# A fifth pair of gate and up products by Strassen's scheme, and ScalarE's casts and first SiLU set one product later

## Chip, core and metric

One NeuronCore of a Trainium2 chip runs the whole model in one launch. The metric is the device time of one execution in microseconds, the median of the timed executions.

Engine names as in the profile: PE is TensorE (matmuls; PEld its weight loads), DVE is VectorE, ACT is ScalarE, POOL is GpSimd, SP is SyncE, which issues loads. Each engine takes its instructions in the order in which the program gives them to it.

## What is computed

Two layers on a sequence of 512 tokens with 1024 features. Each layer is a token mixer (causal pooling in layer 0, differential attention in layer 1), a residual sum with layer norm, a SwiGLU feed-forward, and again a residual sum with layer norm. Only the feed-forward is touched here:

```python
D_FF = 2816
def _swiglu(x, w_gate, w_up, w_down):
    return (jax.nn.silu(x @ w_gate) * (x @ w_up)) @ w_down

x = _layernorm(ALPHA * x + _swiglu(x, w_gate[i], w_up[i], w_down[i]), ln_ffn_g[i], ln_ffn_b[i])
```

All data are float32.

## The kernel before

**Three products for one.** Every operand is split into a high part (ScalarE's cast to the matmul's format) and a low part (VectorE's subtraction of that from the original). A product is high x high + high x low + low x high, three matmuls.

**Gate and up.** The 2816 hidden features are 22 blocks of 128, taken as 11 pairs (k = 0 to 10; block k and block k + 11). A pair needs gate and up for two blocks. It is computed in one of two ways:

- *plain* (function `plain`, once per block): gate and up each take 8 blocks of the inner dimension x 3 matmuls on 512 columns, 96 matmuls for a pair.
- *Strassen* (function `strassen`, pairs listed in `SPLIT`): the pair is a product of 2 x 2 blocks and is done with seven half-size products instead of eight, each of 2 x 4 x 3 = 24 matmuls on 256 columns, 168 for a pair. They come in the order P1, Q5, P6, Q3, P7, P2, Q4. P1, P6, P7 and Q4 add up in bank A of PSUM, Q5 and Q3 in bank C, P2 stands in bank B. Partial results are taken out between products: ScalarE copies P1 to a buffer (L814), Q5 to `second` (L816), P6 to `first` (L818), VectorE subtracts Q3 (L820) and P7 (L822) and adds P2 to the buffer of P1 (L824). ScalarE applies SiLU to that buffer (L825) and to bank A after Q4 (L828); VectorE multiplies with `first` and `second` (L832, L834). The next product that adds to a bank waits until the copy out of it is done. The buffers (`sg`) alternate between two.

**Weights.** A pair has four raw weight tiles of 512 KB, loaded by SP into five buffers (`raw`). A Strassen pair needs seven weight operands: VectorE makes four of them by sums of raw tiles (L552). Then every operand, seven or, for a plain pair, four, is cast (ScalarE, L555) and gets its low part (VectorE, L558); they stand in six pairs of buffers (names g_16h, g_16l and so on, numbered in the order of products; pair 4 begins at g_16). `ahead` after each product prepares the weights some products in front, in the order of the list `steps`.

**Work behind.** Generators in the list `behind` are advanced one step after each product by `catch_up`. There are two kinds:

- `sum_terms` (`weight_sums` starts one per pair, at the places in the tuple of `plain` and at the end of every Strassen pair): sums of blocks of the down weights on VectorE (L657, L658), then two stores to scratch memory by ScalarE's DMA queue (L662), and then GpSimd's loads of later terms (L651, L652).
- `sum_hidden` (once per pair): four VectorE instructions that add and subtract parts of the finished hidden blocks into `u` (L683 to L686), ScalarE's cast of `u` (L687), in the next step VectorE's low part (L689), then a store to scratch (L691).

**Down.** The product with the down weights uses the seven Strassen products over all pairs; its operands come from the hidden blocks and the scratch memory.

Of the kernel before, what the change touches and what calls it, by code (L numbers as in the profile page):

```python
# [43 lines left out]
RAWS = 5  # L44
HALF = FB // 2
DOWN = ("P1", "Q5", "P6", "Q3", "P7", "P2", "Q4")
SPLIT = (4, 6, 7, 9)
GATE = ("P1", "Q5", "P6", "Q3", "P7", "P2", "Q4")
PAIRS = [(0, 2), (2, 2), (4, 2), (6, 2), (8, 2), (10, 1)]

# [2 lines left out]
def trunk(ctx, tc, x, wall, pscale, lam_p, subln, table, lng, lnb, band, first, onehot, out):  # L53
# [395 lines left out]
    def ffn(layer, late):  # L449
# [5 lines left out]
        with tc.tile_pool(name=f"ffn{layer}", bufs=1) as fp:  # L455
# [221 lines left out]
            def sum_hidden(k):  # L677

                first, second = hid[:, k, :256], hid[:, k, 256:]
                a12, a22 = hid[:, k + HALF, :256], hid[:, k + HALF, 256:]  # L680
                u = fp.tile([P, 2, 256], F32, tag="u", name=f"u{layer}_{k}", bufs=1)
                v = fp.tile([P, 2, 2, 256], F32R, tag="v", name=f"v{layer}_{k}", bufs=2)
                tt(u[:, 0, :], first, second, op=ALU.subtract)  # L683
                tt(second, second, a22, op=ALU.subtract)
                tt(u[:, 1, :], a12, first, op=ALU.subtract)
                tt(u[:, 1, :], u[:, 1, :], second, op=ALU.add)  # L686
                nc.scalar.copy(v[:, :, 0, :], u)  # L687
                yield
                tt(v[:, :, 1, :], u, v[:, :, 0, :].bitcast(F32), op=ALU.subtract)  # L689
                yield  # L690
                nc.scalar.dma_start(out=ssum[:, :, :, k, :], in_=v.bitcast(F32))  # L691
# [65 lines left out]
            def plain(f):  # L757
                k = f // 2
                j = index[k] + 2 * (f % 2)
                a = (bank(f"g{layer}_{f}"), bank(f"u{layer}_{f}"))  # L760
                for i in range(2):
                    product(a[i], j + i, 0, S)
                    ahead(j + i + 5)
                    if f >= 3:
                        next(sums, None)
                    catch_up()
                gated(order[f], *a)
                if f < SB:
                    affine(n - 1, f)
                if f in (3, 5, 7, 11, 17):  # L770
                    weight_sums()
                if f == 3:
                    load_terms(3)
                if f % 2:
                    behind.append(sum_hidden(k))

            def strassen(k):
# [12 lines left out]
                def both(t):  # L790
                    return t.rearrange("p (f t) -> p f t", f=2)
# [4 lines left out]
                for j, p in enumerate(GATE):  # L796
# [15 lines left out]
                    if p == "P1":  # L812
                        g0 = tile_of(0)
                        nc.scalar.copy(both(g0), acc)  # L814
                    elif p == "Q5":
                        nc.scalar.copy(second, acc)  # L816
                    elif p == "P6":
                        nc.scalar.copy(first, acc)  # L818
                    elif p == "Q3":
                        tt(first, acc, first, op=ALU.subtract)  # L820
                    elif p == "P7":
                        tt(second, second, acc, op=ALU.subtract)  # L822
                    elif p == "P2":
                        tt(both(g0), acc, both(g0), op=ALU.add)  # L824
                        nc.scalar.activation(g0, g0, AF.Silu)  # L825
                    else:
                        g1 = tile_of(1)
                        nc.scalar.activation(both(g1), acc, AF.Silu)  # L828
                    ahead(index[k] + j + 6)
                    catch_up()  # L830
                    if p == "P2":
                        tt(first, both(g0), first, op=ALU.mult)  # L832
                    elif p == "Q4":
                        tt(second, both(g1), second, op=ALU.mult)  # L834
                weight_sums()
                behind.append(sum_hidden(k))
# [515 lines left out]
```

## Time and profile before

| | us |
|---|---|
| timed runs | 970.91, 968.00, 967.26; median 968.0 |
| profiled execution | 971.13, of which the span of its instructions is 969.2 |
| PE busy | 950.4 (98% of the span) |
| DVE busy | 722.7 (75%) |
| ACT busy | 462.6 (48%) |
| granted TensorE clock, mean | 0.996 of full speed |
| pairs 4 to 10 of gate and up | 131.6 to 279.6 in layer 0, 705.9 to 853.9 in layer 1 |

The profile shows, for every instruction, its start and length, the idle time of its engine before it and what ended that. Three kinds of view are used: groups of waits (who waited for whom, total, times, longest), the chain of work that ended last (followed back from the last instruction to what released it), and busy time by stretch. A row of the last has the stretch in us from the span's start, its length, busy time and count of PE, PEld, DVE, ACT and POOL, the granted clock, the busy share of the DMA engines and GB/s.

### The profile page before, as it was taken

How to read it: one execution, taken by the hardware profiler on the slowest of the kernel's cores; microseconds unless marked ns; L12 is line 12 of the kernel's file. 1: busy time of each engine (PE TensorE's matmuls, PEld its weight loads, DVE VectorE, ACT ScalarE, POOL GpSimd, SP SyncE). 2: the span in 40 equal slices, each digit the busy share in tenths (PEclk: the TensorE clock that was granted, in tenths of full speed). 3: DMA queues.
4: the chain of work that ended last, by engine and by line, in shares of the span. 5: the costliest groups of instructions: out<-in, count | busy, mean ns of one | idle time of the engine just before them, and what ended most of it. 6: DMA issues, size and time to landing. Idle time of an engine off the chain costs nothing.

```text
span 969.2 us, 14409 instructions
## 1 busy us (share of the span) xinstructions
PE 950.4 (98%) x5550; PEld 838.2 (86%) x5550; DVE 722.7 (75%) x1069; ACT 462.6 (48%) x754; POOL 120.5 (12%) x151
## 2 busy tenths in 40 slices
PE   8999999999999999999999999999999999999995
PEld 8898898998988888988888888998898989888884
DVE  6859976786668687688787677779776885577687
ACT  5753343343354456656556553733342543354460
POOL 4311211110000201000000000311211110001102
PEclk9999999999999999999999999999999999999998
DMA  8298887883967974323242222496996884787942
GB/s 220 86 291 269 300 260 254 250 273 125 304 225 236 346 260 153 115 78 86 78 141 76 66 88 87 119 315 210 280 290 198 255 287 145 244 265 272 346 151 87
DMA packets 82242, 197.04 MB, mean 203 GB/s; under 512 B 14804, under 2 KB 26196, under 8 KB 82174
## 3 DMA queue, kind: packets, MB, share of 16 engines
q1 hardware_dynamic: 43052, 115.35, 35.2%
q0 software_dynamic: 15520, 46.14, 17.1%
q10 hardware_dynamic: 23602, 34.63, 10.2%
q8 instruction: 43, 0.70, 0.3%
q14 instruction: 25, 0.20, 0.1%
HBM read 159.38 MB, written 36.72 MB: 202 GB/s over the span
## 4 chain that ended last, share of the span: by engine, by line
PE 89%; DVE 7%; ACT 2%; issue 1%; POOL 1%; POOLq 0%; DVEq 0%; ACTq 0%
PE P L870 13%; PE A L805 7%; PE Q L870 6%; PE g L126 5%; PE u L127 5%; PE g L127 5%; PE u L125 5%; PE u L126 5%; PE g L125 5%; PE C L805 4%; PE s L1060 2%; PE B L805 2%; PE v L125 2%; PE v L126 2%; PE v L127 2%; PE q L126 1%
## 5 line engine op out<-in xcount | busy, mean ns | idle before, releaser
L584 DVE TENSOR_TENSOR hid<-sg,u 128x512 f32<-128x512 f32 x28 | 19.2, 686 | 64.7 <-PE u L127 41.5
L687 ACT CAST v<-u 128x512 fp32r<-128x512 f32 x22 | 13.7, 621 | 103.9 <-DVE u L686 103.9
L107 ACT CAST xs<-hid 128x512 fp32r<-128x512 f32 (+1 forms) x60 | 34.7, 581 | 23.0 <-DVE hid L719 23.0
L108 DVE TENSOR_TENSOR xs<-hid,xs 128x512 fp32r<-128x512 f32 (+1 forms) x60 | 38.4, 641 | 7.8 <-ACT xs L107 7.8
L217 ACT ACTIVATE y<-pt,bT,gT 128x128 f32<-128x128 f32 x96 | 36.0, 455 | 16.8 <-PE pt L212 15.8
L1070 ACT ACTIVATE p<-p,mn 128x128 f32<-128x128 f32 (+3 forms) x64 | 35.4, 553 | 14.9 <-DVE mn L1065 14.9
L552 DVE TENSOR_TENSOR raw<-raw,raw 128x1024 f32<-128x1024 f32 x32 | 39.1, 1220 | 0.3
L651 POOL DMA_DIRECT2D b<-in_wall x20 | 14.0, 705 | 171.8 <-DMA tsum<-b 124.3
L711 POOL DMA_DIRECT2D xs<-ssum x24 | 17.4, 725 | 140.1 <-PE Q L870 118.9
L651 POOL DMA_DIRECT2D hid<-in_wall x24 | 18.8, 827 | 91.6 <-DMA tsum<-hid 46.1
L108 POOL TENSOR_TENSOR sql<-sq,sqh 128x512 fp32r<-128x512 f32 x7 | 9.1, 1294 | 165.3 <-ACT sqh L107 165.3
L1065 DVE CUSTOM_DVE_ANT_0 p<-s,bias 128x128 f32<-128x128 f32 (+3 forms) x64 | 28.1, 485 | 0.0
L174 POOL TENSOR_SCALAR rs<-mv 128x1 f32<-128x1 f32 x16 | 8.1, 509 | 159.6 <-DVE mv L172 159.6
L108 DVE TENSOR_TENSOR xt<-y,xt 128x512 fp32r<-128x512 f32 x24 | 16.1, 685 | 15.4 <-ACT xt L107 15.3
L814 ACT COPY sg<-A 128x512 f32<-128x512 f32 x8 | 4.7, 586 | 42.3 <-PE A L805 42.3
L166 DVE BATCH_NORM_STATS2 st<-res 128x6 f32<-128x512 f32 x32 | 22.2, 695 | 1.1
L652 POOL DMA_DIRECT2D hid<-in_wall x12 | 14.8, 1232 | 54.7 <-DMA hid<-in_wall 49.4
L108 DVE TENSOR_TENSOR heads<-k,heads 128x512 fp32r<-128x512 f32 x8 | 5.5, 693 | 20.2 <-ACT heads L107 20.2
L583 ACT ACTIVATE sg<-g 128x512 f32<-128x512 f32 x28 | 16.6, 592 | 5.6 <-PE g L127 5.6
L600 ACT CAST xs<-hid 128x1024 fp32r<-128x1024 f32 x8 | 8.4, 1052 | 21.3 <-DVE hid L617 11.6
L1084 DVE SCALAR_TENSOR_TENSOR p<-p,sm,p 128x128 f32<-128x128 f32 (+3 forms) x32 | 17.6, 551 | 1.1
L1060 PE MATMUL s<-heads 64*128 64x256 f32 (+2 forms) x192 | 17.9, 330 | 0.0
(1088 smaller groups left out, 3614.3 us busy)
## 6 DMA issues: line engine op xcount, KB each, us to landing
raw<-in_wall SPq DMA_DIRECT2D x122, 512.0 KB, 5.5
r<-tsum SPq DMA_DIRECT2D x40, 512.0 KB, 4.4
hid<-in_wall POOLq DMA_DIRECT2D x36, 512.0 KB, 7.5
b<-in_wall POOLq DMA_DIRECT2D x30, 512.0 KB, 7.4
r<-in_wall SPq DMA_DIRECT2D x30, 512.0 KB, 5.8
tsum<-hid ACTq DMA_DIRECT2D x24, 512.0 KB, 5.9
ssum<-v ACTq DMA_DIRECT2D x22, 512.0 KB, 6.8
tsum<-b ACTq DMA_DIRECT2D x20, 512.0 KB, 3.0
```

The source lines that it names most:

```text
L107: nc.scalar.copy(dst_h, src)
L108: (low or nc.vector).tensor_tensor(dst_l, src, dst_h.bitcast(F32), op=ALU.subtract)
L125: nc.tensor.matmul(acc, ah, bh, start=start, stop=False)
L126: nc.tensor.matmul(acc, ah, bl, start=False, stop=False)
L127: nc.tensor.matmul(acc, al, bh, start=False, stop=stop)
L217: nc.scalar.activation(y[:, k, :], pt[:, k * P : (k + 1) * P], AF.Identity, bias=bT[:, n, kk : kk + 1], scale=gT[:, n, kk : kk + 1],)
L552: tt(t, raws[pair[0]], raws[pair[1]], op=ALU.add)
L651: nc.gpsimd.dma_start(out=t[:, j], in_=src[:, j])
L805: nc.tensor.matmul(o, w[:, c], x[:, kk, :], start=p in ("P1", "Q5", "P2") and f + kk + e == 0, stop=p in ("Q4", "Q3", "P2") and (f, kk, e) ...
L870: nc.tensor.matmul(accs[s], x[:, k, r], y[:, c], start=first and k == 0 and e == 0, stop=last and k == m - 1 and e == 2, skip_group_check= ...
L1060: nc.tensor.matmul(accs[c][:, :wide], a[r, qs], b[r, :wide], start=i == 0, stop=i == 2)
L1070: nc.scalar.activation(p, p, AF.Exp, bias=mn[:, q, c : c + 1], scale=-1.0, accum_out=sm[:, q, c : c + 1],)
```

## The change

One more pair is computed by Strassen's scheme, and the pairs are chosen anew: 4, 5, 6, 8, 9 instead of 4, 6, 7, 9. Plain pairs behind pair 3 are then 7 and 10 instead of 5, 8 and 10. The places of `weight_sums` follow, so that there is still one start per pair. `sum_hidden` gets one more step: ScalarE's cast of `u` is issued one `catch_up` behind VectorE's four instructions. In `strassen` the first SiLU is issued behind the `ahead` and `catch_up` of P2, and the first multiply one product later, just before the second.

```diff
-SPLIT = (4, 6, 7, 9)
+SPLIT = (4, 5, 6, 8, 9)
...
                 tt(u[:, 1, :], a12, first, op=ALU.subtract)
                 tt(u[:, 1, :], u[:, 1, :], second, op=ALU.add)
+                yield
                 nc.scalar.copy(v[:, :, 0, :], u)
                 yield
                 tt(v[:, :, 1, :], u, v[:, :, 0, :].bitcast(F32), op=ALU.subtract)
...
                 if f < SB:
                     affine(n - 1, f)
-                if f in (3, 5, 7, 11, 17):
+                if f in (3, 5, 7, 15):
                     weight_sums()
...
                     elif p == "P2":
                         tt(both(g0), acc, both(g0), op=ALU.add)
-                        nc.scalar.activation(g0, g0, AF.Silu)
                     else:
                         g1 = tile_of(1)
                         nc.scalar.activation(both(g1), acc, AF.Silu)
                     ahead(index[k] + j + 6)
                     catch_up()
                     if p == "P2":
+                        nc.scalar.activation(g0, g0, AF.Silu)
+                    elif p == "Q4":
                         tt(first, both(g0), first, op=ALU.mult)
-                    elif p == "Q4":
                         tt(second, both(g1), second, op=ALU.mult)
```

How the order on the engines moves is shown at a joint, where one Strassen pair follows another. Before there is one joint per layer (pairs 6 and 7), after the change there are three (4-5, 5-6, 8-9).

ScalarE at the joint of pairs 6 and 7, before: from the cast of pair 7's sixth weight operand to the copy of its P6.

```order
L555 CAST g_39h<-raw_1804 128x1024
L555 CAST g_40h<-raw_1578 128x1024
L814 COPY sg_7_0_2001<-A_7_1974 128x512
L662 DMA tsum_536<-b_7_1612 128x2x512 x2
L687 CAST v_6_2013<-u_6_2012 128x2x256
L816 COPY hid_534<-C_7_1975 128x2x256
L555 CAST g_41h<-raw_1836 128x1024
L818 COPY hid_534<-A_7_1974 128x2x256
```

ScalarE at the joint of pairs 4 and 5 after the change, the same piece (line numbers are one higher here):

```order
L555 CAST g_28h<-raw_1417 128x1024
L555 CAST g_29h<-raw_1221 128x1024
L815 COPY sg_5_0_1615<-A_5_1588 128x512
L662 DMA tsum_536<-b_5_1226 128x2x512 x2
L817 COPY hid_534<-C_5_1589 128x2x256
L555 CAST g_30h<-raw_1449 128x1024
L688 CAST v_4_1627<-u_4_1626 128x2x256
L819 COPY hid_534<-A_5_1588 128x2x256
```

The cast of the earlier pair's `u` stood ahead of the copy of Q5 out of bank C; now it stands behind that copy and a weight cast, just ahead of the copy of P6.

VectorE at the end of pair 6, before: from the low part of a weight operand of pair 7 over the addition of P2 (L824) and the two multiplies to the sum of down weights.

```order
L558 TENSOR_TENSOR g_36l<-raw_1578,g_36h 128x1024
L824 TENSOR_TENSOR sg_6_0_1754<-B_6_1729,sg_6_0_1754 128x512
L832 TENSOR_TENSOR hid_534<-sg_6_0_1754,hid_534 128x2x256
L552 TENSOR_TENSOR raw_1578<-raw_1578,raw_1804 128x1024
L558 TENSOR_TENSOR g_38l<-raw_1694,g_38h 128x1024
L834 TENSOR_TENSOR hid_534<-sg_6_1_1961,hid_534 128x2x256
L657 TENSOR_TENSOR b_7_1612<-b_7_1612 128x512
```

VectorE at the end of pair 4 after the change, the same piece:

```order
L558 TENSOR_TENSOR g_25l<-raw_1221,g_25h 128x1024
L825 TENSOR_TENSOR sg_4_0_1368<-B_4_1343,sg_4_0_1368 128x512
L552 TENSOR_TENSOR raw_1221<-raw_1221,raw_1417 128x1024
L558 TENSOR_TENSOR g_27l<-raw_1307,g_27h 128x1024
L834 TENSOR_TENSOR hid_534<-sg_4_0_1368,hid_534 128x2x256
L835 TENSOR_TENSOR hid_534<-sg_4_1_1574,hid_534 128x2x256
L657 TENSOR_TENSOR b_5_1226<-b_5_1226 128x512
```

The first multiply moved behind a weight sum and a low part, next to the second multiply.

## The prediction

> **What bounds the kernel now.** I read the page first: its span, its engine shares, the chain that ended last.
>
> ```profile
> span 969.2 us, 14409 instructions
> PE 950.4 (98%) x5550; PEld 838.2 (86%) x5550; DVE 722.7 (75%) x1069; ACT 462.6 (48%) x754; POOL 120.5 (12%) x151
> PE 89%; DVE 7%; ACT 2%; issue 1%; POOL 1%; POOLq 0%; DVEq 0%; ACTq 0%
> ```
>
> TensorE sets the end nearly everywhere, so only two things can pay: fewer columns on TensorE, or removal of a place where it waits. Next I cut the gate and up stage of the first FFN at the first matmul of each pair from 4 to 10 (a view of busy time by stretch; the first two numbers are the stretch and its length, then busy PE, PEld, DVE and ACT).
>
> ```profile
> 131.63:151.94 20.31, 20.31 (x170) 20.19 (x168) 16.29 (x21) 9.64 (x12) 2.69 (x3) 1.00 1.02 324
> 151.94:173.73 21.79, 21.79 (x99) 18.03 (x97) 12.63 (x16) 6.32 (x8) 2.72 (x3) 1.00 0.74 230
> 173.73:194.04 20.31, 20.31 (x170) 20.19 (x168) 18.27 (x22) 9.02 (x11) 2.70 (x3) 1.00 0.79 237
> 194.04:215.75 21.71, 20.42 (x171) 20.22 (x170) 17.39 (x23) 10.74 (x14) 2.71 (x3) 1.00 0.81 277
> 215.75:237.53 21.78, 21.78 (x98) 18.02 (x97) 12.62 (x16) 6.32 (x8) 0.00 (x0) 1.00 0.49 156
> 237.53:257.85 20.32, 20.32 (x170) 20.20 (x169) 16.04 (x20) 8.70 (x11) 2.35 (x3) 1.00 0.78 275
> 257.85:279.63 21.78, 21.78 (x98) 18.02 (x97) 11.84 (x17) 8.27 (x12) 0.00 (x0) 1.00 0.76 233
> sum 148.02, PE 146.73 PEld 134.90 DVE 105.08 ACT 58.87 POOL 13.13; mean PE 20.96 PEld 19.27 DVE 15.01 ACT 8.41 POOL 1.88
> ```
>
> The last row is the sum of the same seven pairs of the second FFN; the first FFN's seven lengths add up to 148.00 us. Plain pairs (5, 8, 10) take 21.78. Strassen pairs take 20.31, except pair 7, which directly follows another Strassen pair and takes 21.71. What pair 7 loses is in the waits of TensorE and in the chain:
>
> ```profile
> PE C L805 <- ACT hid L816: 2.6, 2, 1.3
> ```
>
> ```profile
> 179.64 2.88 PE A L805 x24
> 182.52 3.06 PE C L805 x24
> ...
> 185.67 0.06 DVE hid L820
> ...
> 194.66 0.64 ACT sg L825
> ...
> 202.51 0.43 DVE u L686
> ...
> 202.97 0.03 ACT v L687
> ...
> 203.50 0.59 ACT hid L816
> ...
> 204.13 3.14 PE C L805 x24
> ```
>
> Product Q3 adds to bank C, so it must wait until ScalarE has copied Q5's result out of it (L816). In ScalarE's queue L816 stands behind the cast L687, which waits for VectorE's L686. VectorE reaches L686 late at a joint of two Strassen pairs, and for 18.5 us (185.67 to 204.13) the chain runs over VectorE. The same wait is small elsewhere: Q3 of pair 6 takes 3.06 instead of 2.88. So an undisturbed Strassen pair would be 7 x 2.88 = 20.16 us.
>
> **The change part by part.** Line numbers are those of before; from L687 on, the changed file is one higher (the second product's multiply L834 becomes L835), the first SiLU L825 becomes L832 and the first multiply L832 becomes L834.
>
> *The fifth Strassen pair.* 96 matmuls of 512 columns (21.78 / 96 = 227 ns each) give way to 168 of 256 (2.88 / 24 = 120 ns each). Per layer 21.78 - 20.16 = 1.62 us less TensorE time, in two layers 3.24. The Strassen pairs become 4, 5, 6, 8, 9.
>
> The Trainium skill, "TensorE: Matmul & The Clock Gate", section "Back-to-back issue gap", gives N / 2.4 + 2.5 ns for a warm matmul. An estimate by that is 96 x 215.8 - 168 x 109.2 = 2.37 us per pair, so 4.7 us in place of 3.24 and a total near 959.2 us. This trace has about 13 ns per matmul above the columns' time instead of 2.5, so the 72 additional matmuls eat more of the gain; the rows above decide.
>
> *The cast L687 one product later.* It now stands behind L816 (second ScalarE listing above). L816 then waits only for Q5's end and for the two DMA issues ahead of it. The wait of pair 7 goes, 21.71 - 20.16 = 1.55 us per layer, 3.10 in two, and the small ones of the other three, 0.15 + 0.15 + 0.16 = 0.46, 0.92 in two. Both assume that nothing else is late in its place, and there are now three joints per layer (4-5, 5-6, 8-9) where there was one. So the joint must be walked with VectorE's own rows.
>
> ```profile
> 185.67:207.38 21.71, 20.42 (x171) 20.22 (x170) 19.36 (x24) 11.26 (x15) 2.71 (x3) 1.00 0.80 245
> ```
>
> ```profile
> 185.67 0.69 DVE L820 TENSOR_TENSOR hid<-C,hid 128x512 f32<-128x512 f32 x1 [1.09 <-PE C L805]
> ...
> 189.81 0.68 DVE L822 TENSOR_TENSOR hid<-hid,A 128x512 f32<-128x512 f32 x1
> ...
> 193.94 0.68 DVE L824 TENSOR_TENSOR sg<-B,sg 128x512 f32<-128x512 f32 x1
> 195.32 0.69 DVE L832 TENSOR_TENSOR hid<-sg,hid 128x512 f32<-128x512 f32 x1 [0.70 <-ACT sg L825]
> 195.93 1.22 DVE L552 TENSOR_TENSOR raw<-raw,raw 128x1024 f32<-128x1024 f32 x1
> 198.20 0.68 DVE L834 TENSOR_TENSOR hid<-sg,hid 128x512 f32<-128x512 f32 x1
> ```
>
> The first row is the cycle from pair 6's L820 to pair 7's: VectorE works 19.36 us in it. The changed joint holds the same 24 instructions, so TensorE's 20.16 us per pair leaves VectorE 0.80 us of slack per joint: tight, but a lag does not add up from joint to joint. With time from the start of the earlier pair, L820 starts at 11.64 (Q3 ends at 4 x 2.88 = 11.52, and the rows start 0.1 later). By the distances of the rows L822 runs from 15.78 to 16.46, and Q4 wants bank A at 6 x 2.88 = 17.28: 0.8 to spare. L824 ends at 20.59.
>
> *SiLU and multiplies later.* VectorE's 0.70 us wait for the SiLU at the joint goes, because it now does a weight sum and a low part (195.93 to 198.20, 2.27) before the first multiply, which then ends at 20.59 + 2.27 + 0.61 = 23.47; the SiLU is ready at about 20.6 + 0.6 = 21.3. This is worth nothing by itself on TensorE; it is what brings L686 forward: its end came 4.74 behind the start of L834 (198.20 to 202.94), at 29.2, and comes at 23.47 + 4.74 = 28.2. It adds one wait: the next pair's copy of P1 (L814) writes the buffer that the first multiply reads, since there are two of them. L814 stood here:
>
> ```profile
> 197.26 1.05 ACT L555 CAST g_40h<-raw 128x1024 fp32r<-128x1024 f32 x1 [0.55 <-DVE raw L552]
> 198.21 0.58 ACT L814 COPY sg<-A 128x512 f32<-128x512 f32 x1
> 200.25 0.37 ACTq L662 DMA_DIRECT2D tsum<-b  x1
> ```
>
> The cast ahead of it needs a buffer that the next pair's P1 frees at 23.04, so it runs from 23.1 to 24.1 and L814 from 24.1 to 24.7, after the multiply's 23.47 anyway. The next P6 needs bank A free at 20.16 + 5.76 = 25.92: 1.2 to spare. Behind L814 stand the DMA issues, which wait for VectorE's L658 and went 2.05 behind the start of L834 (198.20 to 200.25), so at 25.5; then L816, which waits for Q5 (25.92) and ends at 26.7; Q3 starts at 28.80: 2.1 to spare. Then L687 waits for L686 (28.2), and L818 behind it waits for P6's end (28.80) anyway; P7 starts at 31.68. L820 of the next pair is wanted at 31.80, and VectorE is free for it at 11.64 + 19.36 = 31.00. So nothing takes the wait's place, by 0.8 us. Where two joints follow each other (4-5-6) the second repeats the first. After pairs 6 and 9 the SiLU also falls behind a cast, but there VectorE has the work of a plain pair.
>
> *Loads.* The sums read new raw tiles just behind L820. After a plain pair they were issued only a little earlier:
>
> ```profile
> 179.67 0.33 SPq L97 DMA_DIRECT2D raw<-in_wall  x1
> ```
>
> ```profile
> 187.53 1.23 DVE raw L552
> ```
>
> ```profile
> raw<-in_wall SPq DMA_DIRECT2D x1, 512.0 KB, 7.1
> raw<-in_wall SPq DMA_DIRECT2D x7, 512.0 KB, 8.0
> b<-in_wall POOLq DMA_DIRECT2D x3, 512.0 KB, 10.1
> ssum<-v ACTq DMA_DIRECT2D x1, 512.0 KB, 15.4
> ```
>
> The second sum of pair 6 starts at 187.53, and its tile (issued at 179.67, 7.1 us to landing) came 0.8 us before. The rows below it are medians of raw loads around pair 4, of term loads around pairs 6 and 7, and the longest 512 KB transfer around pair 4. The changed joints 4-5 and 8-9 have this tile in the same place (joint 5-6 has its tiles long before). At 8.0 the sum would start 0.1 late; a lateness up to 0.8 is swallowed by bank A's margin. So a landing costs TensorE from 8.7 us on, one us per us, at four joints. I take the raw loads' own row: no cost. Far end: 15.4, (15.4 - 8.7) x 4 = 27 us.
>
> The Trainium skill, "DMA: Bandwidth & Descriptors", section "Issuing engines are not separate DMA queues", says that transfers of all queues interleave on the same 16 engines; the raw loads' 7.1 beside 8.0 in the busier stretch (DMA share 1.02) fit that. By that rule this price hangs on the scratch writes in flight beside, not on SP.
>
> *End of the stage.* VectorE waits there for the last weight terms:
>
> ```profile
> 264.56 0.69 DVE L657 TENSOR_TENSOR b<-b 128x512 f32<-128x512 f32 x1 [2.52 <-DMA b<-in_wall]
> ...
> 279.90 0.69 DVE L584 TENSOR_TENSOR hid<-sg,u 128x512 f32<-128x512 f32 x1 [4.19 <-PE u L127]
> ```
>
> Those terms are loaded once the sum before them has been stored. That sum followed the end of pair 8 (237.53); now it follows the Strassen pair 8, which starts at 131.63 + 3 x 20.16 + 21.78 = 213.9, by 24.1 us: 238.0. So the terms come when they came before, or little earlier, and TensorE is 3.6 us ahead: the wait grows from 2.5 to between 4 and 6. It holds up the next weights and operands of the down stage on VectorE, which were finished 4.19 us before the last row's wait ended, about when TensorE enters the down stage, and of which TensorE takes one item per 2.7 us (12 matmuls of 227 ns). The reserve of 4.19 shrinks to between 1 and 3. No cost; without that cover up to 2 us per layer.
>
> **The sum.** Per layer 5 x 20.16 + 2 x 21.78 = 144.36 instead of 148.00 and 148.02: 3.64 + 3.66 = 7.3 us. By parts: 3.24 + 3.10 + 0.92. The profiled execution took 971.13 (span 969.2) and would take 963.8; it lies 3.1 above the median of the three timed runs, 968.0. From the median: 960.7, I say **961**.
>
> **Rivals.**
> 1. *The small ends remain.* Something still stands late in front of L816: if the copies run only at L686 + cast + copy (28.2 + 0.5 + 0.6 = 29.3 against 28.80), each of six joints loses 0.5 and the 0.92 stays: 7.3 - 0.9 - 3.0 = 3.4, so 964.6. Against it: the new ScalarE order. For it: the DMA issues ahead of L816, which wait for VectorE too.
> 2. *VectorE becomes the bound (slower).* The joint's 19.36 us of VectorE has 0.8 us of room, and the buffer of the first multiply ties the next pair to VectorE's queue. If a joint keeps its present cycle of 21.71, there are three instead of one: per layer 144.36 + 3 x 1.55 + 2 x 0.15 = 149.3, against 148.0, in all 970.6. It decides once VectorE's cycle with its waits exceeds 20.16. For it: today's cycle does. Against it: 21.71 - 19.36 = 2.35 of that cycle is waiting (0.70 for the SiLU, the rest around the late Q3), which the new order takes away.
> 3. *The raw tile lands late.* At 10.1 us, (10.1 - 8.7) x 4 = 5.6 back: 966.3. The gain is gone from 10.5 on; at 15.4 it is 988.
> 4. *The change does not do what it says*: the fifth pair only moves the waits, and the fewer columns alone remain: 968.0 - 3.24 = 964.8.
>
> **How the numbers follow.** Forecast 0.70, rivals 1 and 4 together 0.14, rival 2 0.10, rival 3 0.06. The forecast's own range is 958.5 to 963.5 (the three runs before spread over 3.7). The range of 8 in 10 also takes in rivals 1, 4 and the nearer end of 3: 958 to 967. About 0.5%, 4.8 us, is what a measurement of this kernel can tell from no change. Faster: nearly all of the forecast and a quarter of rivals 1 and 4, 0.71. Slower: the far end of 3 and a worse 2, 0.05. Same: the rest, 0.24.
>
> **What would show it.** Right: the wait of L805 for the copy out of C is gone; Strassen pairs take 20.2 each, Q3 2.88 like the others; VectorE's cycle at a joint is 20.2 with 19.4 busy, and its wait for the SiLU is gone there; the wait for b at the end grows to between 4 and 6. Wrong: TensorE waits at bank A for L814 or L822 (VectorE is the bound), or VectorE waits for a raw tile at the second sum of pairs 4 and 8.

## The result

The changed kernel takes 961.94 us in the median of six runs (960.38 to 964.14); before takes 967.99 in the median of six (967.26 to 970.91). The ratio is 0.9933, with a 95% interval of 0.9911 to 0.9954: 6.1 us less, and the whole interval lies below 1, so it is a gain, if a small one. The forecast was 961, in a range from 958 to 967.

The profiled execution took 960.4, its span is 958.4. Its page begins:

```profile
span 958.4 us, 14744 instructions
PE 942.1 (98%) x5694; PEld 838.9 (88%) x5694; DVE 741.2 (77%) x1089; ACT 473.2 (49%) x766; POOL 120.4 (13%) x151
...
PE 92%; DVE 4%; ACT 1%; POOL 1%; issue 1%; POOLq 0%; DVEq 0%
```

VectorE's share of the chain that ended last fell from 7% to 4%. The same cut of the first feed-forward at the first matmul of pairs 4 to 10 (stretch, length, busy PE, PEld, DVE, ACT, POOL, clock, DMA share, GB/s) now reads:

```profile
128.18:148.33 20.15, 20.15 (x169) 20.15 (x168) 18.18 (x22) 9.22 (x11) 2.69 (x3) 1.00 0.93 267
148.33:168.49 20.16, 20.16 (x170) 20.16 (x169) 19.18 (x24) 10.33 (x13) 2.72 (x3) 1.00 0.85 258
168.49:188.65 20.16, 20.16 (x170) 20.16 (x169) 17.21 (x22) 10.95 (x14) 2.70 (x3) 1.00 0.91 297
188.65:210.44 21.79, 21.79 (x99) 18.02 (x97) 12.63 (x17) 6.31 (x8) 2.70 (x3) 1.00 0.79 236
210.44:230.59 20.15, 20.15 (x169) 20.15 (x168) 18.17 (x22) 9.21 (x11) 0.00 (x0) 1.00 0.49 166
230.59:250.75 20.16, 20.16 (x170) 20.16 (x169) 16.35 (x21) 10.00 (x13) 2.35 (x3) 1.00 0.84 286
250.75:272.54 21.79, 21.79 (x99) 18.02 (x97) 12.47 (x18) 8.16 (x12) 0.00 (x0) 1.00 0.79 262
```

In every row the busy time of PE equals the length: TensorE waits nowhere in the stage. The seven lengths add up to 144.36 us, in the second layer as well, against 148.00 and 148.02: 7.30 us less. The waits of TensorE over the whole program (engine, tile and line, what it waited for: total, times, longest) no longer have the copy out of bank C among them:

```profile
PE warm L273 <- POOL ident masks.py:199: 2.3, 1, 2.3
PE pt L212 <- DVE res L184: 1.8, 3, 1.4
PE pool L322 <- ACT fh L107: 1.0, 1, 1.0
PE g L126 <- DVE xt L108: 0.5, 1, 0.5
PE q L126 <- DVE xt L108: 0.2, 1, 0.2
```

**Where the rest of the difference of the spans comes from.** The two spans differ by 969.2 - 958.4 = 10.8 us, 3.5 more than the two stages. All of it lies ahead of pair 4 of layer 0, where no instruction was changed. The first transposes (L212) began at 31.6 us in the profiled execution of before and at 28.2 in that of the change. The input was there at the same time: the first matmul that works on it (L322) started at 7.55 and at 7.56. But TensorE then went through its matmuls at different speeds. The rows are the same stretch of the token mixer of layer 0, of before and then of the change:

```profile
10.80:18.60 7.80, 7.80 (x32) 6.95 (x32) 4.56 (x7) 4.49 (x7) 4.31 (x3) 1.00 0.89 173
```

```profile
10.80:18.60 7.80, 7.80 (x61) 7.34 (x61) 6.36 (x10) 6.42 (x11) 4.26 (x3) 1.00 0.97 181
```

TensorE is busy for the whole 7.80 us in both, with 32 matmuls in one and 61 in the other: one of 256 columns came every 0.21 us in before and every 0.12 us in the change. The code of this stretch is the same, so the difference belongs to the execution and not to the change; the last section shows it for all kernels. The length of the two stages is therefore the sharper measure, and the timed medians, with their spread of 3 to 4 us, the blunter one.

### The profile page after: what moved, and what is told of

The parts are those of the page before. It is cut to its first block, busy times and chain, and to the rows that moved or that the text cites. A ratio compares the mean times of both kernels' runs of the same rounds, so it can differ in the third digit from the quotient of the medians.

```text
span 958.4 us, 14744 instructions
## 1 busy us (share of the span) xinstructions
PE 942.1 (98%) x5694; PEld 838.9 (88%) x5694; DVE 741.2 (77%) x1089; ACT 473.2 (49%) x766; POOL 120.4 (13%) x151
## 4 chain that ended last, share of the span: by engine, by line
PE 92%; DVE 4%; ACT 1%; POOL 1%; issue 1%; POOLq 0%; DVEq 0%
PE P L871 13%; PE A L806 12%; PE Q L871 6%; PE C L806 6%; PE g L126 5%; PE g L127 5%; PE u L127 5%; PE u L126 5%; PE u L125 5%; PE g L125 5%; PE B L806 3%; PE s L1061 2%; PE v L125 2%; PE v L126 2%; PE v L127 2%; PE q L126 2%
## 5 line engine op out<-in xcount | busy, mean ns | idle before, releaser
L584 DVE TENSOR_TENSOR hid<-sg,u 128x512 f32<-128x512 f32 x24 | 16.5, 686 | 55.5 <-PE u L127 34.6
L552 DVE TENSOR_TENSOR raw<-raw,raw 128x1024 f32<-128x1024 f32 x40 | 48.8, 1220 | 0.3
L583 ACT ACTIVATE sg<-g 128x512 f32<-128x512 f32 x24 | 14.2, 593 | 23.9 <-DVE v L690 15.9
L107 ACT CAST heads<-k 128x512 fp32r<-128x512 f32 x8 | 4.7, 587 | 26.3 <-PE k L127 26.3
```

Of the source, the lines that this page charges most:

```text
L107: nc.scalar.copy(dst_h, src)
L552: tt(t, raws[pair[0]], raws[pair[1]], op=ALU.add)
```

## The experiments

The theory is that of the prediction: a joint of two Strassen pairs costs TensorE a wait at bank C because ScalarE's cast of `u` stands ahead of the copy out of C; the change takes that wait away; VectorE then has 0.8 us to spare per joint. The rivals: the fewer columns alone pay; VectorE is the bound anyway; the raw tile lands late.

All lengths are read at the first matmul of pair 4 and the first of the down product, in both layers. "Between" is from the end of the first stage to the start of the second, "behind" from the end of the second to the end of the span. Times are in us; those of the change come from a separate set of runs with its own runs of before (967.99). The four rows behind the change share one set of runs of before (median 968.37), the next four another (967.96), and the last row has a third (968.41); a ratio is always to the runs of before of the same set.

| kernel | time (lowest to highest) | pair 4 starts | stage, layer 0 | between | stage, layer 1 | behind |
|---|---|---|---|---|---|---|
| before | 967.99 (967.26–970.91) | 131.63 | 148.00 | 426.22 | 148.02 | 115.3 |
| the change | 961.94 (960.38–964.14) | 128.18 | 144.36 | 426.19 | 144.36 | 115.3 |
| fifth pair alone | 971.33 (969.28–974.61) | 130.06 | 149.34 | 426.22 | 149.30 | 115.3 |
| order alone | 964.58 (962.57–967.00) | 131.58 | 145.98 | 426.23 | 145.98 | 115.3 |
| cast alone later | 961.27 (959.88–961.73) | 128.84 | 144.36 | 426.21 | 144.36 | 115.3 |
| SiLU and multiply alone later | 966.91 (964.83–968.80) | 129.87 | 146.95 | 426.18 | 146.93 | 115.3 |
| two more instructions | 960.87 (960.26–964.59) | 131.42 | 144.36 | 426.20 | 144.36 | 115.3 |
| four more instructions | 964.72 (963.76–968.29) | 129.72 | 146.59 | 426.24 | 146.59 | 115.3 |
| pairs 4 to 9 | 958.65 (956.60–960.83) | 131.46 | 142.74 | 426.26 | 142.74 | 115.9 |
| pairs 4 to 10 | 954.32 (953.97–954.79) | 127.79 | 141.11 | 426.27 | 141.11 | 116.1 |
| pairs 4 to 10, old order | 972.05 (972.03–972.93) | 127.74 | 150.51 | 426.21 | 150.50 | 115.3 |

The starts of pair 4 lie between 127.7 and 131.6 and follow no edit; "between" is 426.2 to 426.3 everywhere. "Behind" is 0.6 and 0.8 us longer with pairs 4 to 9 and 4 to 10; that lies behind TensorE's last matmul, and its cause was not followed. (A tile loaded twice and pairs 3 to 10 are told apart below, since their stretches differ.)

### The fifth pair alone

```diff
 (from before)
-SPLIT = (4, 6, 7, 9)
+SPLIT = (4, 5, 6, 8, 9)
...
-                if f in (3, 5, 7, 11, 17):
+                if f in (3, 5, 7, 15):
                     weight_sums()
```

> Part one alone: Strassen pairs 4, 5, 6, 8, 9 and the places of weight_sums, with the cast of u, the first SiLU and the first multiply where they stood before. Theory (the joint): each of the three joints (4-5, 5-6, 8-9) costs what the one joint of before cost, 21.71 - 20.16 = 1.55 us, and the two pairs behind a plain pair (4, 8) keep 0.15. Per layer 144.36 + 3 x 1.55 + 2 x 0.15 = 149.3 us for pairs 4 to 10 against 148.0 before, so the time is 2.6 us above before, some 970.6 beside 968.0; TensorE waits at Q3 for the copy out of C in rows of 1.3 us, six times. Rival (the fewer columns pay by themselves, the joint's wait is one per layer wherever the pairs stand): 148.0 - 1.62 = 146.4 per layer, 964.8. Rival (the five pairs alone bring all of it, the order nothing): 144.4 per layer, 960.7.

Ratio to before 1.0027 (1.0011 to 1.0043): the fewer columns alone make the kernel slower, by 2.6 us in the stages. The stage takes 149.34. The two pairs behind a plain pair lose 0.17 each, so a joint costs (149.34 - 144.36 - 2 x 0.17) / 3 = 1.55 us, as one did before. TensorE's wait is the old one, six times:

```profile
PE C L805 <- ACT hid L816: 7.7, 6, 1.3
```

The rival that only the fewer columns pay is ruled out, and so is the one that the order is not needed.

### The order alone

```diff
 (from the change)
-SPLIT = (4, 5, 6, 8, 9)
+SPLIT = (4, 6, 7, 9)
...
-                if f in (3, 5, 7, 15):
+                if f in (3, 5, 7, 11, 17):
                     weight_sums()
```

> Part two alone: Strassen pairs 4, 6, 7, 9 as before, with the cast of u one step later and the first SiLU and both multiplies in their new places. Theory (the joint): all Strassen pairs take 20.16, per layer 4 x 20.16 + 3 x 21.78 = 145.98 against 148.0, in all 4.0 us less than before, 964.0. Rival (the order alone is worth nothing while VectorE is the bound at the joint): 148.0 per layer, 968. Rival (only the joint's wait goes, the small ends of 0.15 in the other three pairs stay): 146.4 per layer, 964.9; told from the theory by Q3 of pair 6: 2.88 or 3.06.

Ratio 0.9958 (0.9944 to 0.9972); the stage takes 145.98 in both layers, to the hundredth what was expected, and every product on bank C, that of pair 6 too, takes 2.88. The two parts of the change are far from additive: +2.6 us and -4.1 us by the stages, and -7.3 together. The fifth pair turns from a loss into a gain once the order is there.

### The cast alone later

```diff
 (from the change)
                         tt(both(g0), acc, both(g0), op=ALU.add)
+                        nc.scalar.activation(g0, g0, AF.Silu)
...
                     if p == "P2":
-                        nc.scalar.activation(g0, g0, AF.Silu)
-                    elif p == "Q4":
                         tt(first, both(g0), first, op=ALU.mult)
+                    elif p == "Q4":
                         tt(second, both(g1), second, op=ALU.mult)
```

> The change with only the cast of u one step later; the first SiLU and the first multiply stand where they stood before the change. Theory: the cast's place alone removes the wait. VectorE's cycle at a joint is 19.36 busy and 0.70 of waiting for the SiLU, 20.06, just under TensorE's 20.16, so the cast (L686's end 29.2 after the pair's start, cast to 29.7, then the copy of P6 to 30.4) is still ahead of P7 at 31.68. Pairs 4 to 10 take 144.4 us per layer, 960 to 961, the time of the change; VectorE's wait for the SiLU of 0.7 is back and its wait for Q3 at a joint shrinks from 0.81 to about 0.1. Rival (SiLU and multiply are needed, VectorE is over 20.16 without them): up to 0.5 us at each of three joints, 145.9 per layer, 963.5.

Ratio 0.9918 (0.9896 to 0.9940), and the stage takes 144.36: the one `yield` ahead of the cast does all that the new order does for the time. VectorE's rows at joint 4-5 of this kernel (start, length, instruction, in brackets the idle time before it and its releaser):

```profile
140.62 0.69 DVE L821 TENSOR_TENSOR hid<-C,hid 128x512 f32<-128x512 f32 x1 [1.40 <-PE C L806]
...
150.27 0.69 DVE L833 TENSOR_TENSOR hid<-sg,hid 128x512 f32<-128x512 f32 x1 [0.70 <-ACT sg L826]
...
160.78 0.69 DVE L821 TENSOR_TENSOR hid<-C,hid 128x512 f32<-128x512 f32 x1
```

The 0.70 us wait for the SiLU is back, and the wait for Q3 at the end of the cycle is gone: VectorE's cycle fills TensorE's 20.16. Moving the SiLU and the multiply buys VectorE that slack, and nothing that shows in the time.

### SiLU and multiply alone later

```diff
 (from the change)
                 tt(u[:, 1, :], u[:, 1, :], second, op=ALU.add)
-                yield
                 nc.scalar.copy(v[:, :, 0, :], u)
```

> The change with only the first SiLU and the first multiply later; the cast of u stands ahead of the copy out of C as before the change. Theory: L686 ends 28.2 us after the earlier pair's start in place of 29.2, the cast runs to 28.7, the copy out of C to 29.3, and Q3 wants bank C at 28.80: each of three joints loses 0.5 to 0.6 and pairs 4 and 8 about 0.15. Per layer 144.36 + 3 x 0.55 + 2 x 0.15 = 146.3, in all 3.4 us under before, 964.3 to 964.6. Rival (SiLU and multiply are what removes the wait): 144.4 per layer, 960.7. Rival (the cast's place alone decides): 149.3 per layer like part one alone, 970.6.

Ratio 0.9981 (0.9967 to 0.9996). A joint costs (146.95 - 144.36 - 2 x 0.17) / 3 = 0.75 us: half of what it cost in the old order, and more than the 0.55 expected. ScalarE's rows at the joint:

```profile
158.32 0.62 ACT L687 CAST v<-u 128x512 fp32r<-128x512 f32 x1 [3.60 <-DVE u L686]
158.85 0.58 ACT L816 COPY hid<-C 128x512 f32<-128x512 f32 x1
```

The cast waits 3.60 us for VectorE at the head of ScalarE's queue, and the copy out of C stands behind it. The copy ends at 159.43 and Q3 starts at 159.48, 0.65 late; Q3 then takes 2.98 instead of 2.88. These 0.10 were not in the estimate, and L686 came 0.2 later than estimated: it ended 28.4 us behind the pair's start (28.2 expected), against 29.2 in the run with the fifth pair alone. The step that the SiLU's move brings L686 forward holds; without the cast's move these 0.8 us are what it is worth of the 1.55 at each joint.

### How much room VectorE has at a joint

Two kernels add VectorE work behind the second multiply (a maximum of a block with itself, which changes no value). The first adds two instructions of 128x512:

```diff
 (from the change)
                         tt(second, both(g1), second, op=ALU.mult)
+                        for t in (first, second):
+                            tt(t, t, t, op=ALU.max)
```

> The change plus two VectorE instructions of 128x512 per Strassen pair, right behind the two multiplies (the maximum of the product with itself, which leaves every value as it is): 2 x 0.60 = 1.20 us more VectorE work per joint. Theory (0.80 us of VectorE slack per joint, seen as its wait for Q3 in the profile of the change, and then 0.80 of room until bank A is wanted): VectorE lags 0.40 after the first joint and 0.80 after the second of 4-5-6, still inside bank A's room. Pairs 4 to 10 take 144.4 to 144.6 us per layer, the time stays that of the change, 960.4 to 962; VectorE's wait for Q3 at a joint is gone. Rival (VectorE is already the bound at a joint, every us counts): 3 x 1.2 = 3.6 per layer, 148.0, 967.6. Rival (the slack is there but no room behind it): 3 x 0.4, 145.6, 962.8.

960.87, ratio to before 0.9935 (0.9913 to 0.9957), and the stage stays at 144.36: 1.20 us of VectorE work more at every joint cost nothing. VectorE's row L821 at the two ends of joint 4-5:

```profile
143.21 0.69 DVE L821 TENSOR_TENSOR hid<-C,hid 128x512 f32<-128x512 f32 x1 [1.40 <-PE C L806]
163.68 0.68 DVE L821 TENSOR_TENSOR hid<-C,hid 128x512 f32<-128x512 f32 x1
```

The cycle is 20.47; VectorE comes 0.31 late without a cost. So VectorE is not the bound at a joint, and there is room behind its slack. The second kernel adds four:

```diff
 (from the change)
                         tt(second, both(g1), second, op=ALU.mult)
+                        for t in (first, second, first, second):
+                            tt(t, t, t, op=ALU.max)
```

> The change plus four such VectorE instructions per Strassen pair: 2.40 us more per joint, a VectorE cycle of 21.76 against TensorE's 20.16. Theory: the lag after the first joint is 1.60, of which bank A's room takes 0.80, so pair 5 loses 0.8, pair 6 the whole 1.6, pair 9 0.8: 144.36 + 3.2 = 147.6 us per layer, and the time 961 + 6.4 = 967.4; TensorE waits for VectorE (bank A, L823), not for ScalarE's copy out of C. Rival (VectorE is already the bound, every us counts): 3 x 2.4 = 7.2 per layer, 151.6, 975. Rival (VectorE has room beyond what its rows show, or the lag is made up in the pair itself): 144.4, 961.

964.72, ratio 0.9967 (0.9953 to 0.9981). The stage takes 146.59, 2.23 more; 3.2 were expected. TensorE's waits (in the list, one of each kind per layer: bank C at joint 5-6, bank A in pair 5) and ScalarE's row at joint 4-5:

```profile
PE C L806 <- ACT hid L817: 1.2, 2, 0.6
...
PE A L806 <- DVE hid L823: 0.8, 2, 0.4
```

```profile
158.10 0.59 ACT L817 COPY hid<-C 128x512 f32<-128x512 f32 x1 [3.73 <-DVE b L658]
```

The first to give is not bank A but ScalarE's queue again: the copy out of C stands behind a store that waits for VectorE's L658. At this joint Q3 starts 0.23 late and takes 0.10 longer, 0.33 in all. That is the prediction's margin of 2.1 us for L816 (2.40 - 2.1 = 0.3). Bank A (L823) then gives too, for 0.66, but only in pair 5: pairs 6 and 9 are followed by a plain pair, VectorE has no weight sums behind L821 in them, and its lag is gone before L823. At joints 5-6 and 8-9 the copy out of C costs 0.86 and 0.38; the four make the 2.23. The estimate had counted bank A in all three pairs.

### The raw tile loaded twice

```diff
 (from the change)
             nc.sync.dma_start(out=raws[c], in_=wall[c])
+            if c in again:
+                nc.sync.dma_start(out=raws[c], in_=wall[c])
...
+            again.update(c0 + 4 * k + 2 for k in (5, 9))
```

> The change with one raw tile loaded twice at the joints 4-5 and 8-9: the tile of VectorE's second weight sum behind Q3, whose second transfer (same data, same place) starts when the first has landed. Theory: the tile comes some 5 to 6 us later, 12 to 13.5 us after its first issue in place of some 7; from 8.7 on each us costs TensorE one, so each of the four joints loses 3 to 5 us, in all 12 to 20 us, 973 to 981; VectorE's row at the second sum waits for the DMA. Rival (the tile has far more room than 8.7 us, as other work fills VectorE or the operands made are reserves): the time of the change, 961 to 963. Rival (only the transfer's bytes on shared engines matter): 961.

One run: 965.97. One of the four joints loses time, 4-5 of layer 0. There the tile's first transfer was issued at 132.60 (SP's rows), the second could only follow at 138.33, and the second weight sum waited for it:

```profile
132.60 0.33 SPq L99 DMA_DIRECT2D raw<-in_wall  x1
138.33 0.33 SPq L101 DMA_DIRECT2D raw<-in_wall  x1
```

```profile
146.84 1.23 DVE L557 TENSOR_TENSOR raw<-raw,raw 128x1024 f32<-128x1024 f32 x1 [5.26 <-DMA raw<-in_wall]
```

```profile
149.86 0.65 PE L811 MATMUL A<-xt,g_22h 128*128 128x256 f32 x2 [4.45 <-DVE hid L828]
```

VectorE is 5.26 late and TensorE waits 4.45 at bank A: lateness less 0.8, as the prediction had it. At joint 4-5 of layer 1 VectorE began on the tile 9.5 us after its first issue, having waited 0.50, and TensorE did not wait at all; at both joints 8-9 it began 8.9 us after the issue and nobody waited. Only the starting point was off: VectorE wants the tile 146.84 - 5.26 - 132.60 = 9.0 us after its issue, so a landing costs TensorE from 9.8 us on (9.0 and the 0.8 of room), not from 8.7. The expected sum was too large, since two transfers one behind the other took at most 8.9 to 9.5 us at three of the four joints and 14.2 only at this one. Why the second transfer was slow here stays open: from its issue to VectorE's start it took 8.5 us, with the DMA engines busy for 0.92 of the time, and 4.3 us at the same joint of layer 1, with 0.88.

The stage of layer 0 is 150.57, 6.2 longer than in the change, and the wait itself makes 4.5 of it. The rest is told at the end.

### More pairs

Pairs 4 to 9, then 4 to 10:

```diff
 (from the change)
-SPLIT = (4, 5, 6, 8, 9)
+SPLIT = (4, 5, 6, 7, 8, 9)
...
-                if f in (3, 5, 7, 15):
+                if f in (3, 5, 7):
                     weight_sums()
```

> The change with a sixth Strassen pair, 4 to 9 in one row, one plain pair (10) behind; the places of weight_sums follow. Theory: a joint costs nothing since VectorE's lag does not add up (19.36 of 20.16), and the plain pair 7 is not needed for anything to catch up. Per layer 6 x 20.16 + 21.78 = 142.74, 3.24 us less than the change in all: 957 to 958. Rival (the plain pair in between is what lets loads and VectorE catch up; five joints in a row run into late raw tiles): a second sum that waits for its tile for 1 us at the joints 6-7, 7-8 and 8-9 costs some 0.2 to 1 us each, 143.3 to 145.7 per layer, 958 to 963.5. Rival (only as many Strassen pairs pay as the joints are few): 144.4 or more per layer, 961 or above.

The stage takes 142.74, as expected: five joints in a row cost nothing, so the plain pair 7 is not needed for anything to catch up. The time is 958.65, ratio to before 0.9901 (0.9881 to 0.9921), 0.7 above the 957 to 958 expected, which is less than the starts of single executions differ by.

```diff
 (from the change)
-SPLIT = (4, 5, 6, 8, 9)
+SPLIT = (4, 5, 6, 7, 8, 9, 10)
...
-                if f in (3, 5, 7, 15):
+                if f in (3, 5, 7):
                     weight_sums()
...
-                weight_sums()
+                if summed_rows[0] < HALF:
+                    weight_sums()
                 behind.append(sum_hidden(k))
```

> Seven Strassen pairs, 4 to 10, no plain pair behind pair 3; the sums of down weights are all started by the end of pair 9. Theory: pairs 4 to 10 take 7 x 20.16 = 141.12 per layer. But VectorE, which worked 12.47 us in the plain pair 10 of the change and waited 6.12 at its end, gets three to four weight sums, three more low parts and three more small instructions, some 8 us more: 20.5 against 20.16, so the operands of the down stage come some 2 us later than in the change, against a reserve of 6.12. In all 6.5 us less than the change, 954 to 955. Rival (the start of the down stage has no room, its operands are made in pair 10): TensorE waits there for d operands on VectorE or ScalarE, some 2 to 4 us per layer, and the seventh pair brings nothing over the sixth: 957.5 to 962.

This is the best kernel of the study: 954.32, ratio to before 0.9857 (0.9841 to 0.9873), and below the lowest run of the change. One row per layer for the whole stage:

```profile
127.79:268.90 141.11, 141.11 (x1177) 141.11 (x1176) 132.71 (x161) 72.82 (x93) 13.17 (x15) 1.00 0.80 250
695.17:836.28 141.11, 141.11 (x1177) 141.11 (x1176) 132.71 (x161) 72.81 (x93) 13.11 (x15) 1.00 0.78 249
```

VectorE works 132.71 of 141.11 us, and still TensorE has no wait, at the start of the down stage neither ("between" is 426.27). With the old order the same seven pairs are slower than before:

```diff
 (from before)
-SPLIT = (4, 6, 7, 9)
+SPLIT = (4, 5, 6, 7, 8, 9, 10)
...
-                if f in (3, 5, 7, 11, 17):
+                if f in (3, 5, 7):
                     weight_sums()
...
-                weight_sums()
+                if summed_rows[0] < HALF:
+                    weight_sums()
                 behind.append(sum_hidden(k))
```

> Seven Strassen pairs, 4 to 10, with the cast of u, the first SiLU and the first multiply where they stood before the change. Theory (a joint costs 1.55 us in the old order): six joints x 1.55 + 0.15 at pair 4, per layer 141.11 + 9.45 = 150.6 us against 141.11 in the new order and 148.0 before; 954.3 + 18.9 = 973.2, slower than before although TensorE has 9.7 us less to do. Rival (the loss per joint falls when VectorE is late throughout and the pairs stretch): less than 148 per layer, under 968.

972.05, ratio 1.0040 (1.0024 to 1.0056). Each of the six joints costs 1.54, and the wait has grown with their number:

```profile
PE C L805 <- ACT hid L816: 15.5, 12, 1.3
```

So with seven pairs the new order is worth 9.4 us per layer.

The last one begins a pair earlier:

```diff
 (from the kernel with pairs 4 to 10)
-SPLIT = (4, 5, 6, 7, 8, 9, 10)
+SPLIT = (3, 4, 5, 6, 7, 8, 9, 10)
...
-                if f in (3, 5, 7):
+                if f in (3, 5):
                     weight_sums()
```

> Eight Strassen pairs, 3 to 10; the sums of down weights are all started by the end of pair 9. Theory: layer 1 gains another 21.78 - 20.16 = 1.62 us. In layer 0 VectorE works 19.63 us in pair 2 (it makes the sums of x there) and 17.25 in the plain pair 3 of the change; a Strassen pair 3 adds some 8.6 us, 45.5 in the 41.96 us of the two pairs, so VectorE comes 3.5 late, of which 0.8 to 1.6 are swallowed as in the run with four more instructions: TensorE loses about 2 us there and gains 1.62. In all the time of the kernel with pairs 4 to 10 less 1 to 1.6: 952.5 to 954. Rival (the lag of layer 0 is taken up by the reserve of prepared operands): 3.24 less, 951. Rival (the lag stays through the row of Strassen pairs, since their joints leave only 0.8 each): 955 or above.

958.98 (956.87 to 961.18), ratio 0.9897 (0.9878 to 0.9915), slower than pairs 4 to 10 by more than was expected as a gain. In layer 0 pair 3 takes 25.84 us instead of 21.78. TensorE's waits there, and VectorE's first row on bank C:

```profile
PE A L806 <- ACT sg L815: 2.8, 1, 2.8
PE C L806 <- ACT hid L817: 1.1, 1, 1.1
PE A L806 <- DVE hid L823: 0.5, 1, 0.5
PE A L806 <- ACT hid L819: 0.3, 1, 0.3
```

```profile
127.85 0.68 DVE L821 TENSOR_TENSOR hid<-C,hid 128x512 f32<-128x512 f32 x1
```

Pair 3 starts at 109.85, so L821 runs 18.0 us behind it; in step it runs 11.64 behind. VectorE is 6.4 late, not 3.5: the estimate took it as being in step at the start of pair 2 (88.1), but the rows show a lag there already: the SiLU of the block that ended at that moment ran only at 93.98, behind casts of ScalarE that waited for VectorE's sums of x. In layer 1 the pair takes 21.49, a gain of 0.3. VectorE is busy for 45.2 us in pairs 2 and 3 of layer 0, which TensorE could do in 42.0, so it is the bound here. But TensorE's longest wait, 2.8 us, once more comes by way of ScalarE's queue: the copy of P1 stands behind a SiLU and a store that wait for VectorE's L690:

```profile
117.42 0.60 ACT L583 ACTIVATE sg<-g 128x512 f32<-128x512 f32 x1 [3.64 <-DVE v L690]
117.91 0.58 ACT L815 COPY sg<-A 128x512 f32<-128x512 f32 x1
```

In this order pairs 4 to 10 are the limit; whether pair 3 pays with that copy set ahead was not tried.

## Why the prediction was right, and where it was not

**The sum.** 144.36 us per layer was forecast and 144.36 was measured, in both layers. Its terms hold. The fifth pair's 1.62 per layer (a pair at 20.16 for one at 21.78) shows as 145.98 less 144.36 between the order alone and the change; the other estimate of it, 2.37, did not come true. The wait of pair 7 and the small ones of the other three show together as 148.00 less 145.98 = 2.02 per layer (1.55 + 0.46 forecast). What the sum did not hold is the start. The profiled execution took 960.4 and not the 963.8 given for it, because TensorE's speed ahead of pair 4 differed, as told above. The medians differ by 6.1 us and not by 7.3, which lies within the spread of single executions. That the median came within 1 us of 961 is therefore in part luck; that the stages came out to the hundredth is not.

**The joint.** VectorE's and ScalarE's rows at joint 4-5 of the change:

```profile
151.10 0.69 DVE L834 TENSOR_TENSOR hid<-sg,hid 128x512 f32<-128x512 f32 x1
...
156.02 0.43 DVE L686 TENSOR_TENSOR u<-u,hid 128x256 f32<-128x256 f32 x1
...
160.12 0.69 DVE L821 TENSOR_TENSOR hid<-C,hid 128x512 f32<-128x512 f32 x1 [0.81 <-PE C L806]
```

```profile
152.24 0.58 ACT L815 COPY sg<-A 128x512 f32<-128x512 f32 x1
...
154.29 0.59 ACT L817 COPY hid<-C 128x512 f32<-128x512 f32 x1 [1.46 <-PE C L806]
...
156.48 0.62 ACT L688 CAST v<-u 128x512 fp32r<-128x512 f32 x1 [0.66 <-DVE u L686]
157.17 0.59 ACT L819 COPY hid<-A 128x512 f32<-128x512 f32 x1
```

Counted from the start of pair 4 (128.18), the P1 copy runs from 24.06 (24.1 forecast), the copy out of C ends at 26.7 (26.7), L686 at 28.3 (28.2), and VectorE's idle time before L821, in which it waits for Q3, is 0.81 (0.80). The copy L817 now waits for its own product alone.

**The multiply's move "worth nothing by itself".** Right for the change (cast alone later: 144.36). But "it is what brings L686 forward" gave it a part in taking the wait away that it does not need: in the run with the cast alone later L686 ends 29.05 us behind the pair's start, and the joint is free as well. What it buys is VectorE's slack, and half the joint's loss where the cast is not moved.

**Rivals.** VectorE as the bound does not come true at the joints of pairs 4 to 10: 1.2 us more work per joint cost nothing, 2.4 cost 2.2 per layer. It does at pair 3 of layer 0. That an instruction ahead of the copy out of C remains late (the first rival) did not happen, but its place was well chosen: the copy is the first to give when VectorE is made later. The fewer columns alone do not leave 964.8, as the fourth rival had it, but a slower kernel.

**The landing's price.** The mechanism (lateness less 0.8) is right; the start of it at 8.7 us was mis-sized and is 9.8. The forecast took the tile's issue from pair 6 of before, 7.9 us ahead of the sum; in the change with the tile loaded twice it is 9.0 ahead. In the change itself the tile of joint 4-5 of layer 0 landed 5.3 us after its issue, and nobody waited.

**The end of the stage was wrong.** "The wait grows from 2.5 to between 4 and 6", and the reserve "shrinks to between 1 and 3". The wait for the last weight terms shrank to 1.48, and VectorE's idle time ahead of the down stage grew from 4.19 to 6.12:

```profile
257.03 0.69 DVE L657 TENSOR_TENSOR b<-b 128x512 f32<-128x512 f32 x1 [1.48 <-DMA b<-in_wall]
...
272.81 0.69 DVE L584 TENSOR_TENSOR hid<-sg,u 128x512 f32<-128x512 f32 x1 [6.12 <-PE u L127]
```

The step that failed is "so the terms come when they came before". The sum did come when it was said (234.56, with the start of pair 4 lying 3.45 earlier 238.0). But the terms wait for its store, and the store stands in ScalarE's queue. These are ScalarE's rows of before, and then of the change:

```profile
240.66 0.59 ACT L814 COPY sg<-A 128x512 f32<-128x512 f32 x1 [7.05 <-PE A L805]
241.00 0.37 ACTq L662 DMA_DIRECT2D tsum<-b  x1
```

```profile
234.16 0.37 ACTq L662 DMA_DIRECT2D tsum<-b  x1
234.50 0.58 ACT L815 COPY sg<-A 128x512 f32<-128x512 f32 x1
236.01 0.37 ACTq L662 DMA_DIRECT2D tsum<-b  x1
```

Before, the sum was done by 239.8, but its store stood behind the copy of the next pair's P1, which waited for TensorE, and went at 241.0 and 241.5. In the change nothing holds it up: its halves go at 234.16, ahead of the copy, and at 236.01, which is 237.6 and 239.5 if the 3.45 are added. The store goes 2.0 to 3.4 us earlier though the sum is only 0.4 earlier; store and loads were some 2 us shorter besides, and so the wait shrank by 1.0 while VectorE reached it 3 us earlier. It was the same queue that the rest of the prediction was about, and at this place it was not walked. It cost the forecast nothing, because either wait is hidden: TensorE does not wait at the start of the down stage in either kernel.

## What to carry to other kernels

Fewer matmul columns brought nothing here until each place where the accumulation waits for a copy was walked through the queue of the engine that makes the copy: one instruction that waits for a slow neighbour at the head of that queue (here a cast, worth 1.55 us at each joint) turned a saving of 1.62 per pair into a loss, and one `yield` turned it back. Look at which of the instructions ahead of the copy wait for something that the copy itself does not need, and put those behind it. When such a wait is gone, try at once how far the thing it blocked can be taken: five pairs were the change, seven were possible.

When single executions differ by up to 4 us through their start, as here, compare the lengths of the stage that was changed, which agree to 0.02 us, and not the spans.

## What the runs showed of the hardware that was not expected

**A wait of 4.5 us cost 6.2.** In the run with the tile loaded twice, TensorE's granted clock (the column ahead of the last two) fell after its wait. The rows are stretches around it:

```profile
145.30:149.80 4.50, 0.11 (x1) 0.00 (x0) 2.96 (x4) 2.09 (x2) 0.00 (x0) 1.00 0.99 236
149.80:152.70 2.90, 2.84 (x14) 2.85 (x15) 2.87 (x4) 1.04 (x1) 0.00 (x0) 0.54 0.47 155
152.70:155.60 2.90, 2.90 (x23) 2.90 (x23) 2.90 (x4) 1.63 (x3) 0.00 (x0) 0.87 0.56 184
```

In the first stretch behind the wait 14 matmuls went through instead of 24 or so, one every 0.21 us, and it took until 153.5 for them to come at 120 ns again: 6.21 - 4.45 = 1.8 us on top of the wait. After the wait of 2.8 us in the run with pairs 3 to 10 the clock stayed at 1.00:

```profile
118.50:121.40 2.90, 2.86 (x23) 2.86 (x24) 2.87 (x5) 1.10 (x2) 0.00 (x0) 1.00 1.10 273
```

The Trainium skill, "TensorE: Matmul & The Clock Gate", section "HAM oscillation — how this bites in real kernels", says that a gap in TensorE's work of more than about 3.4 us puts it back to half its clock; the two runs agree with it, with 4.45 us on the one side, 2.8 on the other and a clock of 0.54. The prediction's price of one us per us for a late tile therefore does not hold for a wait as long as this one, the only one of its length that these runs have inside the stage.

**The start differs by up to 3.9 us between executions, with TensorE's speed in the first 19 us.** Over eleven kernels with the same opening, pair 4 began between 127.7 and 131.6 us, and the number of matmuls that TensorE did from 7.50 to 18.60 puts them in order: 44 to 46 matmuls where pair 4 began at 131.4 to 131.6, 57 and 59 where it began at 130.1 and 129.9, 71 and 73 at 128.8 and 128.2, 79 and 80 at 127.8 and 127.7. Only the run with four more instructions falls out, with 77 and 129.7; its granted clock was 0.51 later, from 30.6 to 34.1. In the two runs with 57 and 59 the granted clock of the stretch is 0.69. In before it reads 1.00, though the matmuls came every 0.21 us, as they did behind the wait above at 0.54; so this column does not show the slow pace in every trace, and the count of matmuls does. Why TensorE is faster at the start of one execution than of another was not tried and stays open.
